# First layer: two output blocks as standard products and plain values; last layer: one line of linear-attention units with tied reads

## The chip, the cores and the metric

The kernel runs on one core of one Trainium2 chip. The metric is the device time of one execution in microseconds. It is given as the median of several runs; one further execution was taken with the hardware profiler, and the profile page and the trace describe that one.

## The reference

Two layers with the same shape work on 512 tokens of width 2048, all in float32. A layer normalises its rows, multiplies by one wide input matrix, and splits the result into a linear-attention group (4 heads, key width 128, value width 256, a forget gate), a chunked softmax-attention group (8 heads of 128, a relative bias) and a gate for each. The results are normalised for each head, gated, put side by side, multiplied by an output matrix, normalised, and added to the residual.

```
def hybrid_layer(x, w_in, w_out, ...):
    z = rmsnorm(x, g_pre) @ w_in
    gq, gk, gv, gg, ga, aq, ak, av, ag = split_columns(z)
    log_a = log_sigmoid(ga @ w_alpha + b_alpha) / 16
    o_gla = rmsnorm(gla_chunk_causal(gq, gk, gv, log_a), g_gla) * silu(gg)
    o_att = rmsnorm(chunk_band_attention(aq, ak, av, rel_bias), g_att) * silu(ag)
    return x + rmsnorm(concatenate([o_gla, o_att]) @ w_out, g_post)
```

The linear attention keeps a state for each head (128x256). For each chunk of 64 tokens the state is multiplied by a decay and the chunk's outer product of keys and values is added; the chunk's queries then read that new state.

## The kernel before

**Products.** Weights come as blocks of 512 columns: 14 input blocks and 4 output blocks in each layer. Each block is read in 8 chunks of 256 rows, as tiles of 128 x 1024 numbers. A float32 operand is split in a high part, rounded by ScalarE (L257), and a low part, the difference, made by VectorE (L263); a product is three matmuls: high by high, high by low, low by high. Two blocks together form a pair, which is multiplied by a Strassen-Winograd scheme (class `Pair`): seven products P1 to P7 in place of eight, each over 4 chunks. A product of one chunk is 12 matmuls of 128x512 (L523); the query and key pairs run feature-major, 24 of 128x256 (L508). The scheme needs sums of weight tiles (L246, L249, L269, on VectorE, in `Job.high` and `Job.low`) and sums S1 to S4 of the left operand. Those of the input side are made by `token_sums` and read back from memory as `sa`. A pair that is `early` runs P1 and P2 first and reads the lower weight tile again for P4; `second` pairs read their upper tile again for P5. A `seeded` pair copies finished partial results back to PSUM with ScalarE (L453, L547), so that TensorE goes on adding to them; one that isn't seeded combines them with VectorE.

`std_gemm` is the plain alternative: a block is multiplied chunk by chunk, with 6 matmuls for each chunk and each of the four token tiles, and each tile has its own PSUM bank. The last `lag` chunks are ordered tile by tile, so that the banks close one after another. No layer of the kernel before calls it: `PAIRED = (0, 1)` (L138) sends both layers to `paired_out` (L1577 on), which ends `layer`.

**Order of the work in a layer.** Three front pairs (gates and attention values), two query and key pairs with the attention heads beside them, the pair of linear-attention keys and queries, the value pair (`GV0, GV1`, P1 and P2 first), and then the output projection. In `paired_out` this is two pairs, W01 and W23: P1 and P2 of both, then the rest of W01, then the rest of W23. The sums of the output's left operand come from `paired_sums`: S1 and S3 stay in SBUF (`A["S1", c]`), S2 and S4 go through memory (`oS`). Some sums wait until the first output tile is evacuated (`"first"` in `issued`). The last output products are followed by the final rows (`finish_token`, L1557), which in the first layer are transposed (L731) to the next layer's operand by `prep_chunk`. `finish` starts when the low parts of named jobs are made.

**Side work.** Generators in `tasks` are advanced by `pump`, a number of steps after each product (`rate`); `delayed` holds steps to be taken some steps later; `beside(main, other, every)` advances `other` once in `every` steps of `main`. `ahead` loads the weight tiles up to five jobs ahead, fetches left sums up to four ahead, and makes the high and low parts three to four ahead. A scheduler orders the instructions of each engine from this order, and `issue_after(x)` makes an instruction follow `x` on its engine.

**Linear attention.** A `Unit` (L1274) is one head in one half of the tokens (p is 0 or 1). It takes the outer products (`outer`, L1294, four products tied by `issue_after`), the states (`states`, L1314 and L1316 on VectorE), the reads (`read`, L1330, four products, not tied), the norm, the gate (L1348) and the transposes (`turn`, L1358). The profile counts 8 instructions for the four outer products of a unit and 8 for its reads. The last state of a first half is kept in `ends` for the second half. As soon as one half of a value block is done, `gla_heads` takes that block's two heads through that half: four tasks of two units, one after the other, and each task overlaps its two units. The last task carries `paired_sums`.

**Queues.** SP issues the weights, the left operands, and in `load_parts` the sources of the sums; the POOL queue issues what is written to memory, the gain rows, and the residual rows.

Of the kernel before, what the change touches and what calls it, by code (L numbers as in the profile page):

```python
# [35 lines left out]
def hybrid_trunk(  # L36
# [13 lines left out]
    nc = tc.nc  # L50
# [20 lines left out]
    def slot(tag, shape, dtype=F32):  # L71
        return slots.tile([P] + shape, dtype, tag=tag, name=nm(tag))
# [19 lines left out]
    def aux():  # L92
        return ps_ax.tile([P, 512], F32, tag="ax", name=nm("ax"))
# [41 lines left out]
    W01 = (NB_IN, NB_IN + 1)  # L135
    W23 = (NB_IN + 2, NB_IN + 3)
    OUT = (W01[0], W23[0])
    PAIRED = (0, 1)  # L138
    C_IN, C_END = (0, 1, 2, 3), (2, 3, 0, 1)
    MIDDLE = (("P6", 0), ("P3", 0), ("P6", 1), ("P3", 1), ("P6", 2), ("P6", 3), ("P3", 2), ("P3", 3))  # L140

# [36 lines left out]
    class Job:  # L178
# [39 lines left out]
        def bring(self):  # L218
            k, c, p = self.kind, self.c, self.pair
            end = self.b0 in OUT  # L220
            name = LEFT.get(k)
            if self.a is not None:
                return
            src = (so_d if end else sa_d)[self.l].get((name, c))
            if end and name in ("S1", "S3"):
                return
            if src is None or p.get("direct") or p.get("second") and not end and (name, c) in RESIDENT:
                return
            until(lambda: (self.l, end, name, c) in made)
# [42 lines left out]
    for l in range(L):  # L272
        infos = [{"early": True, "direct": True}, {"early": True, "second": True}, {"early": True, "second": True}]
        infos_of.append(infos)
        for k, i in HEAD:
            stream += [Job(l, k, c, *FRONT[i], infos[i]) for c in C_IN]
        for (b0, b1), pr in zip(FRONT, infos):
            stream += [Job(l, k, c, b0, b1, pr) for k, c in early_rest(C_IN)]
        for b0, b1 in PAIRS:
            pr = {"early": b0 == GV0}  # L280
            order = early_head(C_IN) + early_rest(C_IN) if pr["early"] else PROD
            stream += [Job(l, k, c, b0, b1, pr) for k, c in order]
        if l in PAIRED:
# [36 lines left out]
    tasks = []  # L320
# [99 lines left out]
    class Pair:  # L420
# [60 lines left out]
        def operand(self, job, k, c):  # L481
            if job.a is not None:
                return job.a
            if self.end and k in ("P5", "P7"):
                until(lambda: (LEFT[k], c) in A)
                return A[LEFT[k], c]
            if k in ("P1", "P2", "P4") and (self.l, LEFT.get(k), c) not in S_on:
                key = {"P1": (0, 0, c), "P2": (1, 0, c), "P4": (1, 1, c)}[k]
                until(lambda: key in A)
                return A[key]  # L490
            until(lambda: (self.l, False, LEFT[k], c) in made)
            return S_on[self.l, LEFT[k], c]
# [292 lines left out]
    def make_sums(l, end, tags, parts, chunks=range(4), order=None):  # L785
# [4 lines left out]
        def add(name, c):  # L790
            a11, a12, a21, a22 = got[c]
            out, in0, in1, op = {
                "S1": (a22, a21, a22, ALU.subtract), "S3": (a21, a11, a21, ALU.subtract),
                "S2": (a22, a22, a11, ALU.subtract), "S4": (a12, a12, a22, ALU.add),
            }[name]
            with tc.issue_after(last_out[0] or last_state[0]) if end else nullcontext():
                nc.vector.tensor_tensor(out=out, in0=in0, in1=in1, op=op)

        def put(name, c):
# [89 lines left out]
    def layer(l):  # L889
# [379 lines left out]

        og, og_full, issued = {}, {}, {"outer": 0, "states": 0}  # L1270
        last_out[0] = None
        ends = slot("g1" if paired else "g3", [4, 256])

        class Unit:  # L1274
            def __init__(self, h, p, gv):
                self.h, self.p, self.gv, self.i = h, p, gv, issued["outer"]
                st = slot(f"g{9 + self.i % 2}", [4, 256])
                self.st = [st[:, q, :] for q in range(4)]
                if p == 0:
                    self.st[3] = ends[:, h, :]  # L1280
                self.prev = ends[:, h, :] if p else None

            def outer(self):
                h, p = self.h, self.p
# [38 lines left out]
            def read(self):  # L1323
                h, p = self.h, self.p
                self.ps_o = aux()
                for tt in range(2):
                    for cc in range(2):
                        q = 2 * tt + cc
                        n = 4 * p + q
                        nc.tensor.matmul(  # L1330
                            self.ps_o[cc * 64 : (cc + 1) * 64, tt * 256 : (tt + 1) * 256],
                            gqT[h // 2][:, h % 2, n * 64 : (n + 1) * 64], self.st[q],
                            start=True, stop=True,
                        )

            def norm(self):
                ss, self.r = sm(2), sm(2)
# [43 lines left out]
                if ("O", 0) in A:  # L1381
                    A[1, p, h] = op

        def gla_heads(specs):
            units = []

            def new(k):
                h, p = specs[k]
                units.append(Unit(h, p, [gv[h // 2, z] if (h // 2, z) in gv else None for z in range(2)]))
                units[-1].outer()  # L1390

            for _ in range(2 if paired else 4):
                yield
            new(0)
            yield
            units[0].states()
            yield
            for k in range(len(specs)):
                more = k < len(specs) - 1
                if more:  # L1400
# [5 lines left out]
                if more:  # L1406
# [7 lines left out]
                yield  # L1414

        def early_sums():
            while not {(p, h) for p in range(2) for h in (2, 3)} <= set(og):
                yield
            while not paired and issued["states"] < 8:
                yield  # L1420
            yield from output_sums(l, (2, 3))

# [44 lines left out]
                yield  # L1467

        gv = {}
        GV = {(0, 0): "g2", (1, 0): "g4", (1, 1): "g5", (0, 1): "g0"}  # L1470
        passed = set()
        op_att = {}

# [12 lines left out]

        def gv_consume(j, h, t, src, comb):
            if (j, h) not in gv:
                until(lambda: (4 if j or h else 0) in heads_done)
                gv[j, h] = slot(GV[j, h], [2, 512])  # L1490
            dst = gv[j, h][:, t, :]
            if comb is None:
                nc.scalar.activation(dst, src, AF.Copy, scale=inv_rms(l, 2 * h + t))
            else:
                comb(dst)
            if t:
                heads = gla_heads([(2 * j, h), (2 * j + 1, h)])
                if (j, h) == (0, 1):
                    heads = beside(heads, paired_sums(), 2) if paired else beside(heads, early_sums(), 3)
                tasks.append(heads)  # L1500

        values = Pair(l, PAIRS[3], gv_consume, early=True, seeded=True, x_bank=flip ^ 2)
        values.run(early_head(C_IN), rate=4, after=fetch_operands)
        values.open(flip ^ 2)
        values.run(early_rest(C_IN)[:-4], rate=4, after=fetch_operands)
        values.run(early_rest(C_IN)[-4:], rate=4, after=fetch_operands)
        A.clear()

        def operand_out(half, ch):
# [241 lines left out]
```

## Time and profile before

| what | us |
|---|---|
| median of 3 runs | 1634.35 (1633.36 to 1635.29) |
| the profiled execution's own time | 1636.54 |
| its span, first to last instruction | 1634.8 |
| TensorE busy | 1589.1 |
| VectorE busy | 1292.8 |
| ScalarE busy | 948.3 |
| POOL busy | 160.2 |

PE is TensorE's matmuls, PEld its weight loads, DVE is VectorE, ACT ScalarE, and SP the engine that only issues transfers. The profiled execution's own time has 1.7 us outside the span. A row of a view by windows gives the window (us from the start of the span), its length, the busy time and count of each engine, the granted share of TensorE's clock, the mean busy share of the DMA engines, and GB/s. A row of the timeline gives the start, the time taken, the engine, the source line, the operation and how many of them; in brackets is the idle time before it and what ended it. A row of the view of waits gives the total wait, how often, and the longest.

### The profile page before, as it was taken

The page shows a single profiled execution, that of the slowest core. Times are in us where ns is not written, and L with a number is a line of the kernel's source. Part 1 is how long each engine was busy: PE and PEld are TensorE (multiplying, and loading weights), DVE is VectorE, ACT ScalarE, POOL GpSimd, SP SyncE. Part 2 cuts the span into 40 slices and gives each one's busy share as a digit, 9 for nine tenths or more (in the row PEclk, how much of TensorE's full clock was granted, in tenths as well). Part 3 has the DMA queues.
Part 4 walks back from the last instruction along what each step waited for, and adds up shares of the span by engine and source line. Part 5 has one row for each costly group of instructions (what it writes and reads, how often), then busy time and mean ns, then how long its engine had stood idle before and what let it go on. Part 6 is the DMA issues. An engine that isn't in the chain of part 4 may idle for free.

```text
span 1634.8 us, 24266 instructions
## 1 busy us (share of the span) xinstructions
PE 1589.1 (97%) x8722; PEld 1340.2 (82%) x8722; DVE 1292.8 (79%) x1600; ACT 948.3 (58%) x1562; POOL 160.2 (10%) x282
## 2 busy tenths in 40 slices
PE   9999999999999999989899999999999999998896
PEld 6777889999988876767787888899999887766675
DVE  6878976877876787878878888868788767778788
ACT  8565544556676555645585555446657665466343
POOL 1131000000000001110122100000010010010101
PEclk9999999999999999999999999999999999999999
DMA  9999866858867587879769889768586756967795
GB/s 369 357 339 347 326 233 234 300 184 298 278 222 252 206 312 279 288 263 342 260 236 334 324 318 329 258 227 285 191 296 226 259 201 250 367 214 264 274 334 176
DMA packets 144890, 451.57 MB, mean 276 GB/s; under 512 B 15885, under 2 KB 35349, under 8 KB 144769
## 3 DMA queue, kind: packets, MB, share of 16 engines
q1 hardware_dynamic: 124640, 381.07, 66.3%
q0 software_dynamic: 19552, 67.99, 11.1%
q8 instruction: 69, 1.13, 0.3%
q10 hardware_dynamic: 576, 0.95, 0.2%
q14 instruction: 53, 0.43, 0.1%
HBM read 391.44 MB, written 57.43 MB: 275 GB/s over the span
## 4 chain that ended last, share of the span: by engine, by line
PE 78%; DMA 7%; issue 6%; DVE 6%; ACT 1%; POOL 1%; SPq 0%; POOLq 0%; DVEq 0%; ACTq 0%
PE mm L523 48%; PE mm L508 20%; DMA raw<-in_w_dram 3%; DVE wl L263 2%; PE ax L1124 2%; DMA H<-in_w_dram 2%; PE ax L1330 1%; DVE H L246 1%; PE ax L1107 1%; DMA sa<-oS 1%; PE ax L1294 1%; DMA sa<-A 1%; PE ax L1087 1%; PE ax L1086 1%; PE ax L1085 1%
## 5 line engine op out<-in xcount | busy, mean ns | idle before, releaser
L257 ACT CAST wh<-H 128x1024 fp32r<-128x1024 f32 x263 | 276.1, 1052 | 233.5 <-PE mm L523 96.3
L263 DVE TENSOR_TENSOR wl<-H,wh 128x1024 fp32r<-128x1024 f32 (+1 forms) x265 | 321.8, 1217 | 94.0 <-PE mm L523 40.6
L263 DVE TENSOR_TENSOR wl<-raw,wh 128x1024 fp32r<-128x1024 f32 x240 | 292.8, 1220 | 107.4 <-PE mm L523 45.9
L257 ACT CAST wh<-raw 128x1024 fp32r<-128x1024 f32 x240 | 252.5, 1053 | 199.2 <-PE mm L523 92.1
L523 PE MATMUL mm<-wh,sa 128*128 128x512 f32 x1088 | 350.5, 395 | 8.6 <-ACT mm L453 3.8
L523 PE MATMUL mm<-wh,a 128*128 128x512 f32 x1024 | 331.7, 396 | 2.7 <-ACT a L113 1.3
L523 PE MATMUL mm<-wh,g 128*128 128x512 f32 x1024 | 319.8, 391 | 0.2 <-ACT mm L547 0.2
L246 DVE TENSOR_TENSOR H<-H,raw 128x1024 f32<-128x1024 f32 x192 | 233.0, 1220 | 33.3 <-DMA raw<-in_w_dram 22.9
L523 PEld LDWEIGHTS mm<-wh,sa 128*128 128x128 f32 x1088 | 203.7, 189 | 58.4 <-ACT mm L453 5.3
L508 PE MATMUL mm<-sa,wh 128*128 128x256 f32 x1280 | 236.0, 285 | 0.0
L523 PEld LDWEIGHTS mm<-wh,a 128*128 128x128 f32 x1024 | 191.5, 188 | 52.9 <-issue 9.3
L523 PEld LDWEIGHTS mm<-wh,g 128*128 128x128 f32 x1024 | 193.0, 188 | 40.6 <-ACT mm L547 0.9
L523 PE MATMUL mm<-wl,sa 128*128 128x512 f32 x544 | 214.1, 394 | 3.2 <-DVE wl L263 3.2
L523 PE MATMUL mm<-wl,g 128*128 128x512 f32 x512 | 202.2, 395 | 9.9 <-DVE wl L263 9.7
L523 PE MATMUL mm<-wl,a 128*128 128x512 f32 x512 | 201.4, 394 | 1.8 <-DVE wl L263 1.8
L508 PEld LDWEIGHTS mm<-sa,wh 128*128 128x128 f32 x1280 | 199.5, 191 | 0.3
L508 PE MATMUL mm<-sa,wl 128*128 128x256 f32 x640 | 180.7, 283 | 0.0
L523 PEld LDWEIGHTS mm<-wl,g 128*128 128x128 f32 x512 | 96.5, 188 | 36.6 <-DVE wl L263 16.9
L523 PEld LDWEIGHTS mm<-wl,sa 128*128 128x128 f32 x544 | 102.5, 188 | 26.2 <-DVE wl L263 4.6
L508 PEld LDWEIGHTS mm<-sa,wl 128*128 128x128 f32 x640 | 122.3, 191 | 0.1
L523 PEld LDWEIGHTS mm<-wl,a 128*128 128x128 f32 x512 | 96.2, 188 | 24.4 <-DVE wl L263 4.0
L249 DVE TENSOR_TENSOR raw<-H,raw 128x1024 f32<-128x1024 f32 x72 | 87.8, 1219 | 11.1 <-DMA raw<-in_w_dram 10.9
(207 smaller groups left out, 1797.7 us busy)
## 6 DMA issues: line engine op xcount, KB each, us to landing
raw<-in_w_dram SPq DMA_DIRECT2D x360, 512.0 KB, 5.7
sa<-S SPq DMA_DIRECT2D x128, 512.0 KB, 4.6
H<-in_w_dram SPq DMA_DIRECT2D x71, 512.0 KB, 5.9
S<-g POOLq DMA_DIRECT2D x32, 512.0 KB, 5.8
g<-S SPq DMA_DIRECT2D x32, 512.0 KB, 5.2
sa<-A SPq DMA_DIRECT2D x32, 512.0 KB, 6.3
sa<-oS SPq DMA_DIRECT2D x32, 512.0 KB, 5.7
sg<-t POOLq DMA_DIRECT2D x32, 256.0 KB, 5.8
```

Source lines behind the costliest of these rows:

```text
L246: nc.vector.tensor_tensor(out=h, in0=h, in1=r, op=ALU.add)
L249: nc.vector.tensor_tensor(out=r, in0=h, in1=r, op=ALU.subtract)
L257: last_cast[0] = nc.scalar.copy(self.wh, src).ins
L263: last_low[0] = nc.vector.tensor_tensor(out=self.wl[:, kk, :], in0=self.src[:, kk, :], in1=self.wh[:, kk, :].bitcast(F32), op=ALU.subtract ...
L508: nc.tensor.matmul(dst, lhs[:, kk, f], a[:, part, tok], start=(fresh and kk == 0 and m == 0 and ft % 2 == 0), stop=(c == self.last and kk ...
L523: mm = nc.tensor.matmul(out_ps[t], a[:, part, tok], rhs[:, kk, :], start=(fresh and kk == 0 and m == 0), stop=(c == self.last and kk == 1 ...
L1085: nc.tensor.matmul(ps[:, :n], self.qh[:, t], self.kh[:, :n], start=True, stop=False)
L1086: nc.tensor.matmul(ps[:, :n], self.qh[:, t], self.kl[:, :n], start=False, stop=False)
L1087: nc.tensor.matmul(ps[:, :n], self.ql[:, t], self.kh[:, :n], start=False, stop=True)
L1107: nc.tensor.transpose(ps[:, j * P : (j + 1) * P], self.prob[i][:, j * P : (j + 1) * P], ident)
L1124: nc.tensor.matmul(o, self.pt[i][:, j * P : (j + 1) * P], av[hd // 4, j // 2][:, j % 2, (hd % 4) * P : (hd % 4 + 1) * P], start=(j == 0), ...
L1294: mm = nc.tensor.matmul(self.ps_u[cc][:, tt * 256 : (tt + 1) * 256], kd[p][r, tt, hk], self.gv[p][r, tt, hv], start=True, stop=True,).ins
```

## The change

In the first layer:
- `PAIRED` is now `(1,)`, so the output projection goes through the second half of `layer`: block 0 by `std_gemm` over four token tiles, block 1 by `std_gemm` over the first two, then the pair W23 (early, not seeded), then block 1 again over the last two tiles. Block 1's weights are read twice. In the order of the work this puts the second half of block 1 after the pair.
- The left sums are made by `output_sums`: all four go through memory, and their sources are read on SP. The attention operand of the second token half comes through memory, and is read twice.
- The value pair is plain: P1, P5, P6 and P3, P7, P2, P4, with the partial results combined on VectorE.
- `gla_heads` takes one block's two heads through both halves: four units in one chain, heads 2 and 3 after P7, heads 0 and 1 after P4. Heads 0 and 1 thus run beside block 0.

In the last layer:
- One generator, `gla_line`, takes all eight units in the order in which their values come. In each turn it issues a new unit's outer products and then the older unit's reads; `paired_sums` runs beside it from the start.
- The four reads of a unit are tied by `issue_after`, as the outer products already are.

```diff
-    PAIRED = (0, 1)
+    PAIRED = (1,)
...
-            if end and name in ("S1", "S3"):
+            if end and self.l in PAIRED and name in ("S1", "S3"):
...
-            pr = {"early": b0 == GV0}
+            pr = {"early": b0 == GV0 and l in PAIRED}
...
-            with tc.issue_after(last_out[0] or last_state[0]) if end else nullcontext():
+            with tc.issue_after(last_state[0]) if end else nullcontext():
...
                 self.ps_o = aux()
+                mm = None
                 for tt in range(2):
                     for cc in range(2):
...
-                        nc.tensor.matmul(
+                        with tc.issue_after(mm) if paired and mm else nullcontext():
+                            mm = nc.tensor.matmul(
...
-        def gla_heads(specs):
+        def gla_heads(j, gv):
             units = []
             def new(k):
-                h, p = specs[k]
+                h, p = 2 * j + k // 2, k % 2
...
+        def gla_line():
+            n, older = 0, None
+            while n < 8 or older is not None:
+                newer = None
+                if units_due:
+                    h, p = units_due.pop(0)
+                    newer = Unit(h, p, [gv.get((h // 2, z)) for z in range(2)])
+                    newer.outer()
+                    n += 1
+                elif older is None:
+                    yield
+                    continue
+                yield
+                if older is not None:
+                    older.read()
+                yield
+                if newer is not None:
+                    newer.states()
+                yield
+                if older is not None:
+                    older.norm()
+                yield
+                yield
+                if older is not None:
+                    older.gate()
+                    delayed.append([4, older.turn])
+                yield
+                yield
+                older = newer
...
         def early_sums():
             while not {(p, h) for p in range(2) for h in (2, 3)} <= set(og):
                 yield
-            while not paired and issued["states"] < 8:
-                yield
...
-            if t:
-                heads = gla_heads([(2 * j, h), (2 * j + 1, h)])
-                if (j, h) == (0, 1):
-                    heads = beside(heads, paired_sums(), 2) if paired else beside(heads, early_sums(), 3)
-                tasks.append(heads)
+            if t and paired:
+                if (j, h) == (0, 0):
+                    tasks.append(beside(gla_line(), paired_sums(), 2))
+                delayed.append([2, lambda: units_due.extend([(2 * j, h), (2 * j + 1, h)])])
+            elif h and t:
+                heads = gla_heads(j, [gv[j, p] for p in range(2)])
+                tasks.append(heads if j else beside(heads, early_sums(), 3))
...
+        if paired:
+            values = Pair(l, PAIRS[3], gv_consume, early=True, seeded=True, x_bank=flip ^ 2)
...
+        else:
+            fast_gemm(l, PAIRS[3], gv_consume, rate=4, after=fetch_operands, x_bank=flip ^ 2)
```

More of the change, by code (lines that the diff above doesn't have):

```diff
@@ L483, in operand @@
                 return job.a
-            if self.end and k in ("P5", "P7"):
+            if self.end and self.l in PAIRED and k in ("P5", "P7"):
                 until(lambda: (LEFT[k], c) in A)
@@ L1271, in layer, with __init__ @@
         last_out[0] = None
-        ends = slot("g1" if paired else "g3", [4, 256])
+        ends = slot("g1", [4, 256]) if paired else None
         class Unit:
-            def __init__(self, h, p, gv):
+            def __init__(self, h, p, gv, prev=None):
                 self.h, self.p, self.gv, self.i = h, p, gv, issued["outer"]
@@ L1278, in __init__ @@
                 self.st = [st[:, q, :] for q in range(4)]
-                if p == 0:
+                self.prev = prev.st[3] if prev else None
+                if paired and p == 0:
                     self.st[3] = ends[:, h, :]
-                self.prev = ends[:, h, :] if p else None
+                elif paired:
+                    self.prev = ends[:, h, :]
             def outer(self):
@@ L1329, in read @@
                         n = 4 * p + q
[L1330 to L1334, printed above, removed]
+                        with tc.issue_after(mm) if paired and mm else nullcontext():
+                            mm = nc.tensor.matmul(
+                                self.ps_o[cc * 64 : (cc + 1) * 64, tt * 256 : (tt + 1) * 256],
+                                gqT[h // 2][:, h % 2, n * 64 : (n + 1) * 64], self.st[q],
+                                start=True, stop=True,
+                            ).ins
             def norm(self):
@@ L1382, in turn @@
                     A[1, p, h] = op
-        def gla_heads(specs):
+        def gla_heads(j, gv):
             units = []
             def new(k):
-                h, p = specs[k]
-                units.append(Unit(h, p, [gv[h // 2, z] if (h // 2, z) in gv else None for z in range(2)]))
+                h, p = 2 * j + k // 2, k % 2
+                units.append(Unit(h, p, gv, units[-1] if p else None))
                 units[-1].outer()
-            for _ in range(2 if paired else 4):
+            for _ in range(4):
                 yield
@@ L1397, in gla_heads @@
             yield
-            for k in range(len(specs)):
-                more = k < len(specs) - 1
-                if more:
+            for k in range(4):
+                if k < 3:
                     new(k + 1)
@@ L1405, in gla_heads @@
                 yield
-                if more:
+                if k < 3:
                     units[k + 1].states()
@@ L1414, in gla_heads @@
                 yield
+        units_due = []
+        def gla_line():
[27 more added lines that the diff above has]
+                older = newer
         def early_sums():
             while not {(p, h) for p in range(2) for h in (2, 3)} <= set(og):
-                yield
-            while not paired and issued["states"] < 8:
                 yield
@@ L1469, in layer @@
         gv = {}
-        GV = {(0, 0): "g2", (1, 0): "g4", (1, 1): "g5", (0, 1): "g0"}
+        GV = {(0, 0): "g2" if paired else "g0", (1, 0): "g4", (1, 1): "g5", (0, 1): "g0" if paired else "g1"}
         passed = set()
@@ L1488, in gv_consume @@
             if (j, h) not in gv:
-                until(lambda: (4 if j or h else 0) in heads_done)
+                until(lambda: (4 if j or h or not paired else 0) in heads_done)
                 gv[j, h] = slot(GV[j, h], [2, 512])
@@ L1495, in gv_consume @@
                 comb(dst)
-            if t:
-                heads = gla_heads([(2 * j, h), (2 * j + 1, h)])
-                if (j, h) == (0, 1):
-                    heads = beside(heads, paired_sums(), 2) if paired else beside(heads, early_sums(), 3)
-                tasks.append(heads)
[L1502 to L1506, printed above, removed]
+            if t and paired:
[7 more added lines that the diff above has]
+            values = Pair(l, PAIRS[3], gv_consume, early=True, seeded=True, x_bank=flip ^ 2)
+            values.run(early_head(C_IN), rate=4, after=fetch_operands)
+            values.open(flip ^ 2)
+            values.run(early_rest(C_IN), rate=4, after=fetch_operands)
+        else:
+            fast_gemm(l, PAIRS[3], gv_consume, rate=4, after=fetch_operands, x_bank=flip ^ 2)
         A.clear()
```

## The prediction

> **What bounds the kernel now.** I read the page's busy times first, then the chain of waits, then the stretches of single weight products, and then the waits inside the stretches that were too long.
>
> ```profile
> span 1634.8 us, 24266 instructions
> PE 1589.1 (97%) x8722; PEld 1340.2 (82%) x8722; DVE 1292.8 (79%) x1600; ACT 948.3 (58%) x1562; POOL 160.2 (10%) x282
> ```
>
> TensorE is busy 97% of the span. What one product matmul costs is read from the chain where nothing else interferes:
>
> ```profile
> 882.19 81.91 PE mm L523 x360
> 964.55 92.48 PE mm L523 x408
> ```
>
> 92.48 / 408 = 0.2267 us for each 128x512 matmul. A product of one chunk is 12 of them (2.72 us), one product over its four chunks 48 (10.9 us). With this ruler each stretch of the first layer's output projection can be compared with its work. The next rows count the line 523 matmuls alone; the columns are the window, its length, PE busy (count), weight loads (count), granted clock, DMA share and GB/s. The first five are the first layer, the last three the same places in the last layer.
>
> ```profile
> 686.80:702.00 15.20, 11.86 (x49) 8.81 (x48) 1.00 0.61 225
> 702.00:729.50 27.50, 23.73 (x98) 17.74 (x97) 1.00 0.89 326
> 751.20:764.80 13.60, 11.62 (x50) 8.80 (x49) 1.00 1.02 411
> 764.80:797.40 32.60, 32.60 (x145) 27.01 (x144) 1.00 0.83 271
> 797.40:818.80 21.40, 11.41 (x50) 8.80 (x48) 0.92 0.68 255
> 1493.70:1510.40 16.70, 12.25 (x50) 8.79 (x49) 1.00 0.64 237
> 1510.40:1538.80 28.40, 24.45 (x97) 18.83 (x96) 0.94 0.86 318
> 1562.80:1578.10 15.30, 12.79 (x50) 10.11 (x49) 0.89 0.90 356
> ```
>
> (A count one or two over 48, 96 or 144 is a neighbour's matmul at the edge.) The window 764.80:797.40 has no loss: 144 x 0.2267 = 32.6. The first has P5 of pair W01, 48 matmuls in 15.2 us instead of 10.9: 4.3 lost. P6 and P3 of W01 lose 27.5 - 21.8 = 5.7. P5 of W23 loses 13.6 - 10.9 = 2.7. Together 12.7 us. The last layer loses 5.8 + 6.6 + 4.4 in the same three places, so the cause is in the way a paired projection works. Who is waited for in the first layer between 686 and 765, and how busy VectorE is there (PE, PEld, DVE, ACT, POOL):
>
> ```profile
> PE mm L523 <- DVE wl L263: 5.7, 5, 1.5
> PE mm L523 <- ACT mm L453: 1.9, 1, 1.9
> PE mm L523 <- DMA sa<-oS: 1.3, 1, 1.3
> 686.80:729.50 42.70, 35.58 (x146) 26.55 (x145) 34.97 (x39) 20.08 (x28) 5.37 (x10) 1.00 0.79 290
> 729.50:764.80 35.30, 33.32 (x146) 26.78 (x145) 33.39 (x35) 19.52 (x30) 2.67 (x5) 1.00 0.91 327
> ```
>
> VectorE is busy 68.4 of 78 us: it makes the low parts and the weight sums, and the sums of the left operand, all at once. TensorE waits for it, for the scalar copies that seed the banks (L453), and for operands from memory. The stretch 797.40:818.80 is the way into the second layer:
>
> ```profile
> 808.80 1.47 PE L731 MATMUL ax<-cst,g 128*128 128x128 f32 x12
> 815.60 3.39 PE L731 MATMUL ax<-cst,g 128*128 128x128 f32 x16 [5.33 <-DVE g L741]
> ```
>
> Here TensorE has no products left and waits 5.33 us for the normalised rows; then 16 transposes take 3.39 us, 0.21 each, where the 12 before took 0.12 each. That is the lower clock (0.92 mean in this window): another 1.7 us. So 7.0 us go at the border of the layers.
>
> **The change, part by part.**
>
> *Two blocks standard in layer 0.* A pair is 7 products x 4 chunks x 12 = 336 matmuls for two blocks; standard, a block is 8 chunks x 4 token tiles x 6 = 192, two are 384. So 48 matmuls are added: 48 x 0.2267 = +10.9 us. Nothing can hide them, since TensorE is the queue they stand in. The Trainium skill (Perfetto Trace Analysis, Identifying the Most-Contended Engine) says that matmul busy time is a poor measure of headroom and that weight-load busy share is a better one. By that rule the 82% would leave 18% of the span, and the sum would lose its +10.9 term. The trace does not bear that out here: in the full window 764.80:797.40 the loads are 27.0 of 32.6 us (83%), and the pitch stays at 0.2267, so this way gets no chance of its own.
>
> *What that takes away.* The W01 pair's weight sums (P5, P6, P7 and P4, four chunks each) and four low parts go:
>
> ```profile
> L246 DVE TENSOR_TENSOR H<-H,raw 128x1024 f32<-128x1024 f32 x192 | 233.0, 1220 | 33.3 <-DMA raw<-in_w_dram 22.9
> ```
>
> 20 x 1.22 = 24.4 us less on VectorE, and no seeds in this projection. The left sums S1 to S4 spread over block 0 and the first half of block 1 instead of 80 us of pairs. I take the 10.0 us of W01's stalls as gone, and the 2.7 of W23's P5 too (its weight loads double no more: the pair is no longer the "second" one): -12.7. It would stay at 0 if the same wait returned at the new pair; that is a rival.
>
> *The border.* The last step is now the second half of block 1, 96 matmuls = 21.8 us after the new pair's P4, and the first two token rows are finished and transposed during it. Before, only P7's tail and P4 stood over that work. The wait of 5.33 us and the half clock after it have more than twice the cover, so -7.0. If the cover failed, 7.0 would come back whole.
>
> *What memory must carry.* This is the term with no row of its own, since standard blocks don't run in the kernel before. The sizes and latencies:
>
> ```profile
> raw<-in_w_dram SPq DMA_DIRECT2D x360, 512.0 KB, 5.7
> sa<-oS SPq DMA_DIRECT2D x32, 512.0 KB, 5.7
> oS<-g POOLq DMA_DIRECT2D x16, 512.0 KB, 5.0
> a<-fa SPq DMA_DIRECT2D x8, 256.0 KB, 4.3
> t<-in_g_post_dram POOLq DMA_DIRECT2D x12, 256.0 KB, 6.3
> fg<-t POOLq DMA_DIRECT2D x8, 256.0 KB, 6.0
> ```
>
> From block 1's first half to its second, TensorE has 96 + 336 + 96 matmuls, 119.7 us, and some 3.4 us of transposes: 123 us. In them fall 40 weight tiles (21.0 MB), 16 left sums read (8.4), 8 written (4.2), the sources of the last 8 (8 x 256 KB, 2.1), the attention operand fetched a second time (2.1), the residual rows (4.2), four gain rows (1.0) and half of x_mid (2.1): 45.1 MB, less about 2 MB of residual rows that start in block 0. That is 43 / 123 = 350 GB/s of demand. The nearest row is the first layer's front, where weights, columns and sums move together; below it a stretch with less traffic:
>
> ```profile
> 83.70:175.10 91.40, 89.83 (x386) 71.25 (x385) 1.00 0.92 334
> 893.20:1056.90 163.70, 163.70 (x724) 135.54 (x723) 140.02 (x133) 91.85 (x112) 14.67 (x27) 1.00 0.86 305
> ```
>
> In the first, 384 matmuls are 87.0 us of work in 91.4, and 30.5 MB over 87.0 us is a demand of 351 GB/s: 4.4 us lost. In the second, 720 matmuls are 163.2 of 163.7: nothing lost at 305. Scaled, 4.4 / 87.0 x 123 = +6.2 us of new stalls. The bounds: nothing, if the 411 GB/s of 751.20:764.80 were available throughout (45.1 MB in 110 us); 15 us, if all of it went at the 326 GB/s of 702.00:729.50 (138 us). The Trainium skill (DMA: Bandwidth & Descriptors, Where 436 GB/s comes from) has the memory side bind at about 358 GB/s for a core. By that the term would be 45.1 / 0.358 - 123 = +3; the 411 row is above that limit, so the trace doesn't confirm it as a ceiling.
>
> *Queues.* Layer 0's sources are now read on SP, whose next entries are weights. A source waits for the linear attention's write (fg, 6.0 us). In block 0 a weight tile lasts 24 x 0.2267 = 5.4 us and four are buffered, so this costs nothing there; in block 1 (2.7 us a tile, 10.9 buffered) at most a couple of us, inside the bounds above. S1 and S3 go through memory as S2 and S4 do now. The final units of heads 0 and 1 now run in block 0, whose last two chunks need them: 33 us after its start, plus the units' own matmuls. Their pipeline of 34 to 39 steps at 1.7 steps per 1.36 us is done about then, each unit a chunk ahead of its use: nothing, and a few us if the last unit is late.
>
> *Values plain in layer 0.* Same 336 matmuls, four weight loads less, no seeds. The key and query pair already runs in this order. Nothing, either way under 1 us.
>
> *Last layer.* The reads (L1330) of a unit are now tied in order, as the outer products (L1294) already are. Rows of both:
>
> ```profile
> 567.46 2.00 PE L1294 MATMUL ax<-g,g 64*128 64x256 f32 x16
> 575.32 1.94 PE L1330 MATMUL ax<-g,g 128*64 128x256 f32 x14
> 1442.98 0.49 PE L523 MATMUL mm<-wh,a 128*128 128x512 f32 x1
> 1443.41 0.65 PE L1330 MATMUL ax<-g,g 128*64 128x256 f32 x2
> 1443.99 0.49 PE L523 MATMUL mm<-wl,a 128*128 128x512 f32 x1
> ```
>
> In a burst a read takes 0.12 us (575.32 row: 13 steps from first to last start in 1.56). Split in twos, 1442.98 to 1443.99 holds one product and two reads, 0.47 of work in 1.01 us: a break costs about 0.5. In the last layer two units are split in four and two are split once, 3 + 3 + 1 + 1 = 8 breaks too many: 8 x 0.44 = -3.5 us, taking a little under the row. One line of eight units takes 7 steps a unit where two overlapping units took 16 steps; the last unit comes about 7 steps, 1.75 chunks or 5 us, later. The sums of chunks 0 and 1 wait anyway for the first output tile, 12 chunks into the projection, so I cost that at nothing; if sums are pushed into the busy stretch 1493.70:1538.80, up to +3. Bounds -4 to +3.
>
> **Sum**, against the profiled execution's own 1636.54 us: +10.9 - 12.7 - 7.0 + 6.2 - 3.5 = -6.1, so 1630.4. The median of the runs is 2.2 us under the profiled one, so 1628 us, 0.4% faster. About 0.2% (3.3 us) is what can be told from no change here.
>
> **The rivals.** (1) *Memory becomes the bound of layer 0's last three steps.* For it: the demand of 350 is over every long stretch of the trace, and writes and 256 KB pieces are mixed in. Against: 411 GB/s for 13.6 us. If 315 GB/s is what it gets (between the 305 and 326 rows), 45.1 MB take 143 us, the term is 20 instead of 6.2, and the sum is +7.7: 1642. It turns the result to slower than before once the term passes 12.3, so below 333 GB/s. (2) *The stalls only move.* The new pair still makes sums, low parts and evacuations together, with its partial results now combined by VectorE rather than seeded; the front of the last layer shows such pairs running without loss, W23's P5 shows one that doesn't. If half of the 12.7 stays, the sum is +0.3 and the time 1634.6. (3) *The line doesn't do what it says:* ties order the reads but products still come between, and the later last unit costs 3 us. Then -3.5 becomes +3, the sum +0.4, and the time 1635. The unbroken outer products, tied the same way, speak against it.
>
> **How the numbers follow.** Forecast (faster by over 3.3 us) 0.50; rivals 2 and 3, and half measures between, 0.20 within 3.3 us; rival 1 and what of block 0's late units may add to it 0.30. Low end: no new stall and -4 in the last layer, 10.9 - 12.7 - 7.0 - 4 = -12.8: 1621.5. High end: rival 1, 1642.
>
> **What would show it.** Right: two stretches of standard products in layer 0, 192 and 96 matmuls at 0.2267, then the pair, then 96 more; no wait of over 1 us for L263 in them; no 5 us wait before L731 and no clock drop there; L1330 in eights in the last layer; from the first layer's values to the second layer's first product about 2.6 us less than before (10.9 - 12.7 - 7.0 + 6.2). Wrong: long waits of line 257, 246 or the standard matmuls for weights or oS, with a DMA share over 0.9 at 315 GB/s or less; the last layer's losses of 5.8, 6.6 and 4.4 us grown.

## The result and the profile after

The new kernel takes 1620.28 us (median of 4 runs, 1620.19 to 1621.84), against 1634.82 for the kernel before in the same comparison: ratio 0.9911, 95% interval 0.9894 to 0.9928, or 14.5 us less. The forecast was faster, 1628, with a low end of 1621.5: the direction is right, and the time is 1.2 us under the low end of the range. The profiled execution's own time is 1620.26. The head of its page, and the shares of its chain of waits (the second fence has the kernel before's):

```profile
span 1618.5 us, 24386 instructions
PE 1585.6 (98%) x8770; PEld 1347.6 (83%) x8770; DVE 1275.7 (79%) x1590; ACT 934.7 (58%) x1548; POOL 174.2 (11%) x292
PE 88%; issue 4%; DMA 4%; DVE 2%; ACT 1%; POOL 0%; SPq 0%; POOLq 0%; DVEq 0%; ACTq 0%
```

```profile
PE 78%; DMA 7%; issue 6%; DVE 6%; ACT 1%; POOL 1%; SPq 0%; POOLq 0%; DVEq 0%; ACTq 0%
```

There are 48 matmuls more, and TensorE's share of the chain has gone from 78% to 88%: what went is waiting. Where it went, from the timelines of TensorE in the two profiles:

| stretch | before, us | after, us | difference |
|---|---|---|---|
| start to the first layer's value pair | 535.9 | 534.5 | -1.4 |
| value pair to the second layer's first product | 282.9 | 269.9 | -13.0 |
| from there to the last layer's value pair | 522.7 | 523.1 | +0.4 |
| from there to the end of the span | 293.3 | 291.0 | -2.3 |

The first and third rows hold work that is unchanged. Over all the profiles shown here they run from 534.0 to 537.6 and from 522.3 to 525.6, so a difference of 2 or 3 us in these rows means nothing. The second row is steadier: it is 269.9 in all six profiles that have this first layer unaltered. The 13.0 us are the first layer's change. The view by windows of the new kernel, in the first layer: block 0 with the units of heads 0 and 1, the first half of block 1, the pair from P5 to P4, and everything from block 1's first half to the next layer (PE, PEld, DVE, ACT, POOL, clock, DMA share, GB/s):

```profile
625.00:681.10 56.10, 56.10 (x281) 42.61 (x280) 36.43 (x63) 27.98 (x63) 17.86 (x29) 1.00 0.81 285
681.10:702.90 21.80, 21.80 (x98) 18.03 (x97) 16.78 (x20) 11.48 (x15) 2.25 (x5) 1.00 1.04 398
724.70:779.10 54.40, 54.40 (x242) 45.06 (x241) 49.11 (x51) 29.06 (x39) 8.90 (x6) 1.00 0.93 345
681.10:804.40 123.30, 123.30 (x561) 102.42 (x561) 104.26 (x118) 73.26 (x108) 17.28 (x25) 1.00 0.91 344
```

TensorE is never idle in them. In the second and third rows 96 matmuls in 21.8 us and 240 in 54.4 are 0.227 us each. VectorE is still 90% busy in the pair (49.1 of 54.4), but nothing waits for it. At the border the same two groups of transposes as before now stand like this in TensorE's timeline:

```profile
784.10 1.47 PE L731 MATMUL ax<-cst,g 128*128 128x128 f32 x12
790.42 1.91 PE L731 MATMUL ax<-cst,g 128*128 128x128 f32 x16
```

There is no idle time before the 16, and they take 0.12 us each instead of 0.21, so the lower clock is gone too.

The last layer has a new wait, just before P5 of pair W01. The view of waits, the line 523 matmuls by windows (P2, P5, P6 and P3 of W01; P5 of W23), POOL's timeline, and VectorE's:

```profile
PE mm L523 <- DVE g L1573: 4.1, 1, 4.1
```

```profile
1464.50:1480.20 15.70, 11.48 (x50) 8.80 (x48) 1.00 0.92 321
1480.20:1494.10 13.90, 13.12 (x48) 10.13 (x49) 0.88 0.30 115
1494.10:1525.30 31.20, 23.98 (x97) 18.89 (x97) 0.89 0.78 287
1547.30:1561.90 14.60, 11.81 (x50) 8.80 (x49) 1.00 1.02 402
```

```profile
1461.20 0.71 POOL L582 TENSOR_TENSOR sm<-sm,cst 128x2 f32<-128x2 f32 x1 [2.48 <-ACT sm L586]
1462.06 1.13 POOL L1560 DMA_DIRECT2D t<-in_g_post_dram  x2
```

```profile
1479.35 1.28 DVE L1573 TENSOR_TENSOR g<-mm,t 128x512 f32<-128x512 f32 x2
```

P2 loses 4.8 us. P5 adds into the banks that hold W23's first output tile. That tile is complete at 1464.5, but VectorE multiplies it by its gain row, and so empties the banks, only at 1479.35. The gain row was asked for at 1462.06, on POOL's queue right behind the last unit's norm (L582), and such a row lands about 5.8 us later. So the row is there by about 1468; for the other 11 us VectorE has other work in front of the evacuation, weight sums and low parts above all.

### The profile page after: what moved, and what is told of

The parts are those of the page before. It is cut to its first block, busy times and chain, and to the rows that moved or that the text cites. A ratio compares the mean times of both kernels' runs of the same rounds, so it can differ in the third digit from the quotient of the medians.

```text
span 1618.5 us, 24386 instructions
## 1 busy us (share of the span) xinstructions
PE 1585.6 (98%) x8770; PEld 1347.6 (83%) x8770; DVE 1275.7 (79%) x1590; ACT 934.7 (58%) x1548; POOL 174.2 (11%) x292
## 4 chain that ended last, share of the span: by engine, by line
PE 88%; issue 4%; DMA 4%; DVE 2%; ACT 1%; POOL 0%; SPq 0%; POOLq 0%; DVEq 0%; ACTq 0%
PE mm L523 52%; PE mm L508 20%; PE mm L394 5%; PE ax L1124 2%; DMA raw<-in_w_dram 2%; DMA H<-in_w_dram 1%; DVE wl L263 1%; PE ax L1296 1%; PE ax L1107 1%; PE ax L1334 1%; PE ax L523 1%; PE ax L717 1%; PE ax L1087 1%; PE ax L1086 1%; PE ax L1085 1%
## 5 line engine op out<-in xcount | busy, mean ns | idle before, releaser
L263 DVE TENSOR_TENSOR wl<-H,wh 128x1024 fp32r<-128x1024 f32 (+1 forms) x253 | 307.8, 1219 | 93.2 <-PE mm L523 38.6
L523 PE MATMUL mm<-wh,g 128*128 128x512 f32 x928 | 289.2, 391 | 4.1 <-DVE g L1573 4.1
L523 PE MATMUL mm<-wh,a 128*128 128x512 f32 x864 | 279.3, 396 | 3.0 <-ACT a L113 1.1
L246 DVE TENSOR_TENSOR H<-H,raw 128x1024 f32<-128x1024 f32 x176 | 213.8, 1222 | 27.4 <-DMA raw<-in_w_dram 18.9
L523 PEld LDWEIGHTS mm<-wh,g 128*128 128x128 f32 x928 | 175.0, 189 | 40.7 <-issue 4.5
L523 PEld LDWEIGHTS mm<-wh,a 128*128 128x128 f32 x864 | 161.5, 188 | 42.8 <-issue 4.3
L523 PE MATMUL mm<-wl,g 128*128 128x512 f32 x464 | 182.1, 393 | 4.2 <-DVE wl L263 4.2
L523 PE MATMUL mm<-wl,a 128*128 128x512 f32 x432 | 169.6, 394 | 1.2 <-DVE wl L263 1.2
L523 PEld LDWEIGHTS mm<-wl,a 128*128 128x128 f32 x432 | 81.2, 188 | 19.9 <-DVE wl L263 3.3
L508 PE MATMUL mm<-a,wh 128*128 128x256 f32 x512 | 94.5, 285 | 0.0
```

The costliest lines, as they stand in the source:

```text
L246: nc.vector.tensor_tensor(out=h, in0=h, in1=r, op=ALU.add)
L263: last_low[0] = nc.vector.tensor_tensor(out=self.wl[:, kk, :], in0=self.src[:, kk, :], in1=self.wh[:, kk, :].bitcast(F32), op=ALU.subtract ...
L508: nc.tensor.matmul(dst, lhs[:, kk, f], a[:, part, tok], start=(fresh and kk == 0 and m == 0 and ft % 2 == 0), stop=(c == self.last and kk ...
L523: mm = nc.tensor.matmul(out_ps[t], a[:, part, tok], rhs[:, kk, :], start=(fresh and kk == 0 and m == 0), stop=(c == self.last and kk == 1 ...
```

## The experiments

**The first layer alone** (`first_only`). The last layer gets back the four tasks of two units, with the reads not tied:

```diff
-                if (j, h) == (0, 0):
-                    tasks.append(beside(gla_line(), paired_sums(), 2))
-                delayed.append([2, lambda: units_due.extend([(2 * j, h), (2 * j + 1, h)])])
+                heads = gla_pairs([(2 * j, h), (2 * j + 1, h)])
+                tasks.append(beside(heads, paired_sums(), 2) if (j, h) == (0, 1) else heads)
...
-                        with tc.issue_after(mm) if paired and mm else nullcontext():
+                        with tc.issue_after(mm) if False else nullcontext():
```

> The first layer changed as in the new kernel, the last layer as before: its value halves start pairs of units, reads not tied. Theory: the first layer alone brings nearly all, 13.0 us between its value pair and the next layer's first product (10.9 more work, 12.8 less waiting in the projection, 6.9 less at the border, 4.4 less for the linear-attention units, and no new wait for memory), so 1621 to 1622 us, ratio 0.992. Rival: the first layer brings only the 2.6 us that the prediction gave it and the last layer the rest, so about 1632 us, ratio 0.998.

Measured: 1617.67 us, ratio 0.9906 (0.9889 to 0.9922). The first layer's change alone brings all of the gain.

**The last layer alone** (`last_only`). The kernel before, with `gla_line` and the ties in the last layer.

```diff
+            if t and last:
+                if (j, h) == (0, 0):
+                    tasks.append(beside(gla_line(), paired_sums(), 2))
+                delayed.append([2, lambda: units_due.extend([(2 * j, h), (2 * j + 1, h)])])
...
```

> The first layer as before (both output pairs paired, values early), the last layer with the one line of units and tied reads. Theory: 1.5 to 2.5 us faster, about 1632.5 us, ratio 0.9985: some 4 us less for the units and a new wait of 4 to 5 us before P5 of pair W01, partly given back after it. Rival: the last layer brought what the first did not, 10 us or more, about 1623 us.

Measured: 1633.64 us, ratio 1.0011 (0.9998 to 1.0024). It isn't faster, so the theory's small gain fell with the rival. In its profile the units cost the last layer less, and P2 of W01 loses 3.7 us, where the kernel before lost 0.2.

**Ties without the line** (`first_ties`). As the first kernel, but with `if paired and mm` left in.

> The first layer changed, the last layer with the old pairs of units but tied reads: the line is left out. Theory: the reads come in eights, which saves the breaks, 3 to 4 us, and since the last unit is not later the wait before P5 of pair W01 is not there: 1617 to 1619 us, 2 to 3 us under the kernel with the line. Rival: the line and not the ties is what saves the breaks: 1621.5 us, as with the first layer alone.

Measured: 1615.65 us, ratio 0.9897 (0.9880 to 0.9914). But this is no second kernel. It builds to the same program as the one without ties, so the 2.0 us between the two are what two samples of one program differ by. The last layer's reads, still tied, in TensorE's timeline:

```profile
1426.97 0.65 PE L1334 MATMUL ax<-g,g 128*64 128x256 f32 x2
1427.97 0.65 PE L1334 MATMUL ax<-g,g 128*64 128x256 f32 x2
1428.97 0.65 PE L1334 MATMUL ax<-g,g 128*64 128x256 f32 x2
1429.97 0.65 PE L1334 MATMUL ax<-g,g 128*64 128x256 f32 x2
```

They come in twos, as before: a tie sets an order, which the reads had anyway, and lets products in between. The new kernel with its ties taken out also comes to the same program. So the ties do nothing. In the first layer, with no ties at all, the reads of the new kernel come in eights. There the chain of four units issues them at another time; that this is the reason is argued, not shown:

```profile
607.18 1.14 PE L1296 MATMUL ax<-g,g 64*128 64x256 f32 x8
608.24 1.08 PE L1334 MATMUL ax<-g,g 128*64 128x256 f32 x8
615.60 1.14 PE L1296 MATMUL ax<-g,g 64*128 64x256 f32 x8
616.66 1.08 PE L1334 MATMUL ax<-g,g 128*64 128x256 f32 x8
```

**Standard blocks with the old values and units** (`first_early`). The kernel before, with `PAIRED = (1,)` and only what that needs:

```diff
-            if end and name in ("S1", "S3"):
+            if end and self.l in PAIRED and name in ("S1", "S3"):
...
-            if self.end and k in ("P5", "P7"):
+            if self.end and self.l in PAIRED and k in ("P5", "P7"):
...
```

> The kernel before with only the two output blocks of the first layer made standard: its values stay early and seeded, its units stay in four tasks of two. The last layer is as before. Theory: the blocks bring 10.9 - 12.8 - 6.9 = -8.8 us, and the 4.4 us of cheaper units come from the chain of four units with the plain values, so they are missing: 1626 us, ratio 0.9945. Rival: the units are cheaper because half of them now run beside a standard block, whatever the order of the values: 1621 to 1622 us, ratio 0.992.

Measured: 1621.80 us, ratio 0.9932 (0.9912 to 0.9953). From the value pair to the second layer its profile has 273.7 us: 9.2 less than before, 3.8 more than the new kernel. The blocks bring 9 us, and plain values with chains of four, which weren't tried apart, bring the other 4, as the theory said. The intervals of this ratio and of `first_only`'s overlap, so the split rests on the profiles.

**The border** (`unsplit`). Block 1 of the first layer runs once, over all four token tiles, before the pair, and the first rows are finished from P7 on:

```diff
-        std_gemm(l, NB_IN + 1, (0, 1), OO, operand_out, out_evac(1), rate=0.6, lag=2)
+        std_gemm(l, NB_IN + 1, range(NT), OO, operand_out, out_evac(1), rate=0.6, lag=1)
...
-        std_gemm(l, NB_IN + 1, (2, 3), OO, operand_out, last_evac, ...)
...
```

> The new kernel, but in the first layer block 1 is multiplied once over all four token tiles, before the pair, so the pair is the last step; the first rows are finished from P7 on, as in the kernel before. Theory: the standard products behind the pair are what covers the border. Without them the wait before the transposes and the lower clock come back, 5 to 7 us: 1625 to 1627 us. Rival: the border is short because the pair no longer runs with the sums beside it; then the time stays at 1620 us or falls a little, since 8 weight tiles and 4 operand tiles less are read.

Measured: 1626.59 us, ratio 0.9936 (0.9912 to 0.9960), about 4 us over the new kernel's ratio, with intervals that overlap. The time lies in the theory's range, but the mechanism doesn't hold: in the profile the way from the value pair to the second layer is 271.5 us, only 1.6 longer than in the new kernel. The window of P4, now the last step, and the 16 transposes:

```profile
791.70:807.30 15.60, 15.02 (x81) 12.24 (x80) 15.60 (x20) 9.42 (x17) 5.57 (x5) 1.00 0.96 352
```

```profile
805.02 1.91 PE L730 MATMUL ax<-cst,g 128*128 128x128 f32 x16
```

TensorE is busy 15.0 of 15.6 us. There is no 5 us wait and no lower clock, though nothing but the pair covers the border. The window is 15.6 us where the kernel before took 21.4. So most of the border's 7 us doesn't come from the 96 matmuls that were put there.

**The border's other cause** (`before_gains`). The kernel before, with one gain row of each pair, in both layers, asked for earlier:

```diff
-                    elif (k, c) == ("P4", C_END[0]):
+                    elif (k, c) == ("P7", C_END[0]):
                         gains[n] = load_gain(n, nc.gpsimd)
```

> The kernel before with one thing moved: in both layers' paired projections the gain row that each pair's P4 needs is asked for 4 products earlier, after P7's first chunk instead of P4's. Theory: at the border TensorE waits 5.33 us because VectorE stands at a gain row that was asked for at 807.06 and is used at 813.12; with the row there, the transposes follow at once, the lower clock does not come, and 5 to 7 us go at the border: 1627 to 1630 us. Rival: the border is long because nothing but P4 covers the last rows; then the wait only changes its name and the time stays within 2 us.

Measured: 1627.82 us, ratio 0.9963 (0.9949 to 0.9977): 6 us faster than the kernel before, with one request moved in each of four pairs. Its transposes at the border:

```profile
800.60 1.47 PE L731 MATMUL ax<-cst,g 128*128 128x128 f32 x12
806.95 1.03 PE L731 MATMUL ax<-cst,g 128*128 128x128 f32 x8
808.75 1.03 PE L731 MATMUL ax<-cst,g 128*128 128x128 f32 x8
```

The idle time is gone, and from P4 to the second product of the next layer the loss is 6.4 us instead of 13.2; in the new kernel it is 6.3. What held the border was the gain row: VectorE stood at it for 1.9 us, and the evacuation that the transposes needed was queued behind. The standard form asks for those rows on SP, before the pair. That this is what makes the border short in the new kernel and in `unsplit` is the likely reading; no run delays the request there. The result bears on the whole change. From the value pair to the second layer this profile has 273.3 us, as short as the 273.7 of `first_early`: in this stretch the paired blocks with their gain rows in time do as well as the standard ones, without 48 more products. The whole time isn't as good (ratio 0.9963 against 0.9932, intervals that overlap a little), and no run joins the moved request to the other parts of the change.

**More traffic** (`mem2`). Each of the 8 left sums of chunks 0 and 1 in the first layer is written twice more, to memory that nothing reads:

```diff
...
+            if end and l == 0 and c in (0, 1):
+                for _ in range(2):
+                    nc.gpsimd.dma_start(spare_d.pop(), flat(op))
```

> The new kernel with two more writes, to scratch memory that nothing reads, of each of the 8 left sums of chunks 0 and 1 in the first layer: 16 more transfers of 512 KB, 8.4 MB, between block 0 and the last standard step. Theory: memory still had room; the stretch carried 42.4 MB in 123.3 us (344 GB/s) without a wait, and its first 21.8 us ran at 398 GB/s; 50.8 MB need 123 us at 412 GB/s, so a loss of 0 to 5 us. Rival: the limit is near 350 GB/s and the new kernel stands at it; then 8.4 MB cost 24 us, 1644 us.

Measured: 1638.37 us, ratio 1.0014 (1.0002 to 1.0027), 17 us over the new kernel's ratio. Both expectations missed. The windows from block 1's first half on, and the whole stretch:

```profile
682.90:704.60 21.70, 21.70 (x97) 18.00 (x96) 16.71 (x20) 11.53 (x15) 5.29 (x10) 1.00 1.04 405
704.60:729.60 25.00, 21.97 (x97) 17.84 (x96) 15.04 (x18) 11.85 (x20) 6.41 (x13) 0.99 1.03 416
729.60:747.20 17.60, 14.66 (x48) 10.61 (x49) 12.88 (x12) 5.14 (x5) 1.07 (x2) 0.83 1.03 418
682.90:819.80 136.90, 129.10 (x561) 103.31 (x560) 105.06 (x118) 72.91 (x108) 20.32 (x40) 0.98 0.95 369
```

For 64 us memory moves 405 to 418 GB/s at a share of 1.03 to 1.04, and TensorE starts to wait 22 us in. The stretch is 13.6 us longer (136.9 to 123.3). So the ceiling is above 400, not near 350, and the new kernel runs its 123 us at 344 under it. Its first half of block 1 ran at 398 and a share of 1.04 without any wait of TensorE, so even a full memory need not cost time at once. The 13.6 us need not be the price of 8.4 MB alone. ScalarE waits 4.7 us, before it makes a sum, for one of the added writes, which points at a buffer that the write still reads; and TensorE's longest wait here, of 3.0 us, is for ScalarE:

```profile
ACT g L114 <- DMA spare<-g: 4.7, 1, 4.7
PE mm L524 <- ACT wh L258: 3.0, 1, 3.0
```

The two costs were not tried apart. The Trainium skill (Perfetto Trace Analysis, Roofline) gives about 435 GB/s as the ceiling of a single core's 16 DMA engines, with 358 as the share when two cores read. The trace fits the first, since the one core here moved 418.

**The last layer's gain rows** (`gains_first`).

```diff
+                    if (n, k, c) == (0, "P1", C_END[0]):
+                        gains[2], gains[0] = load_gain(2, nc.gpsimd), load_gain(0, nc.gpsimd)
                     if (n, k, c) == (0, "P1", C_END[3]):
-                        gains[2], gains[0] = load_gain(2, nc.gpsimd), load_gain(0, nc.gpsimd)
```

> The new kernel with the first two gain rows of the last layer's projection asked for at the first product of pair W01 instead of its fourth. Theory: the wait of 4.5 us before P5 of pair W01 is for the bank that the pair W23's first output tile holds; that tile is evacuated 15 us late because its gain row was asked for behind the last unit's norm on the POOL queue. With the row there in time the wait goes, and the time falls by 2 to 5 us, to 1615 to 1618 us. Rival: VectorE's own queue holds the evacuation back, whatever the row; then nothing changes, 1620 us.

Measured: 1618.04 us, ratio 0.9884 (0.9867 to 0.9901), 4.4 us under the new kernel's ratio; the two intervals overlap a little, but this one lies clear of the second measurement of the new kernel below (0.9907 to 0.9938). P2, and then P6 and P3 of W01, and the wait in the latter:

```profile
1465.40:1476.80 11.40, 11.32 (x50) 8.97 (x49) 1.00 0.82 276
1492.30:1527.20 34.90, 25.52 (x97) 20.18 (x96) 0.83 0.70 258
```

```profile
PE mm L523 <- DMA sa<-oS: 9.4, 1, 9.4
```

The wait before P5 is gone (11.4 us for 48 matmuls, 0.5 lost), as the theory said. Part of it comes back as a wait for a sum that goes through memory. Here too asking for the gain row earlier removes the wait, though the row was not what VectorE stood at: with the earlier request VectorE takes the evacuation at 1471.87, ahead of weight work that it did first in the new kernel. The second wait was not followed further.

**The line against the tasks, again** (`new_again`, `first_again`; no edit).

> The new kernel once more, beside the next one on the same chip, to set the last layer's line apart. Theory: the line saves some 4 us of breaks in the last layer and gives them back in the later wait before P5 of pair W01, so this and the kernel with the first layer changed alone lie within 3 us of each other. Rival: the line costs or brings more than 3 us.

> The first layer changed alone, once more. Theory: within 3 us of the new kernel, 1616 to 1620 us. Rival: more than 3 us away from it.

Measured on one chip: 1621.68 us, ratio 0.9923 (0.9907 to 0.9938), with the line; 1616.18 us, ratio 0.9894 (0.9875 to 0.9914), without. That is 4.7 us apart, outside the theory's 3 us, but the intervals overlap, and the first two measurements of these kernels (0.9911 and 0.9906) were 0.8 us apart by the ratios. The profiles tell more. Without the line, P2, P5, P6 and P3 of W01 and P5 of W23 stand like this, and the gain rows are asked for earlier:

```profile
1466.00:1476.80 10.80, 10.80 (x49) 8.97 (x48) 1.00 0.73 237
1476.80:1494.20 17.40, 13.47 (x50) 9.86 (x50) 0.90 0.61 230
1494.20:1520.30 26.10, 23.22 (x98) 17.81 (x97) 1.00 0.88 335
1542.00:1556.30 14.30, 11.84 (x50) 8.82 (x49) 1.00 1.02 403
```

```profile
1458.96 1.17 POOL L1590 DMA_DIRECT2D t<-in_g_post_dram  x2 [0.35 <-DMA raw<-in_w_dram]
```

P2 loses nothing, with the rows asked for 7.0 us before W23's P2 ends, where the line had 2.4. From the last value pair to the end, the three profiles without the line (`first_only`, `first_ties`, `first_again`, one program) have 286.5, 286.6 and 286.6 us; with it, 291.0 and 293.0. The line's value pair with its units is cheaper by some 3 us, and the waits behind it cost 7 to 9 more. So the line costs 4 to 6 us there.

**Both layers in the new form** (`both_std`).

```diff
-    PAIRED = (1,)
+    PAIRED = ()
```

> The last layer takes the first layer's new form too: two output blocks standard, plain values, units in chains of four. Theory: the last layer's paired projection still loses 22.6 us in waits, which the standard form does not have; it costs 10.9 us of products, and the end of the kernel keeps its tail: 1607 to 1613 us, 8 to 12 us under the new kernel. Rival: the last layer has no next layer to cover, and with no paired sums its tail after the last products grows: no gain, 1620 us or more.

Measured: 1605.24 us, ratio 0.9802 (0.9784 to 0.9821): 30 us under the kernel before and 18 under the new one by the ratios, more than the theory gave it. This beats both kernels. From the last value pair to the end it takes 274.9 us, against 286.5 in `first_only`. The head of its page, and the last layer: values and block 0, then the first half of block 1 with the pair, and the last half:

```profile
span 1603.0 us, 24514 instructions
```

```profile
1418.50:1474.70 56.20, 56.20 (x282) 42.63 (x281) 36.50 (x63) 27.84 (x63) 17.86 (x29) 1.00 0.80 285
1474.70:1572.60 97.90, 97.90 (x433) 81.11 (x432) 83.04 (x89) 51.95 (x70) 13.13 (x12) 1.00 0.94 350
1572.60:1594.50 21.90, 21.90 (x97) 17.84 (x95) 14.37 (x16) 7.21 (x11) 1.63 (x3) 1.00 0.46 161
```

TensorE is busy without a gap to its last product, and the end behind it is 8.5 us.

## Why the prediction was right and wrong, step by step

- *Two blocks standard, +10.9 us.* Right. The 384 matmuls run at 0.2267 us, and none was hidden.
- *W01's stalls and W23's P5, -12.7 us.* Right. No product of the first layer's projection waits, and block 0 needed no margin for the late units. With the border this gives -8.8 for the blocks; `first_early` has -9.2. Against the paired form with its gain rows in time (`before_gains`) the trade is about even: there the same places lose 11.2 us.
- *The border, -7.0 us.* The size is right (10.5 us over the products in P4's stretch before, 3.6 after, all transposes). The reason is wrong, so the size is luck: the prediction had "more than twice the cover". `unsplit` has no such cover and no such wait, and `before_gains` removes the wait in the kernel before by asking for one row earlier. The row was in the wait list (VectorE waits 1.9 us for `t<-in_g_post_dram`), and the prediction stopped one step short of it, at the transposes' wait for VectorE. It also didn't ask where the standard form requests it.
- *What memory must carry, +6.2 us.* This is the step that failed first. The demand was right: 350 GB/s worked out, 344 measured. The price was wrong: it measured 0. The prediction scaled "4.4 us lost" at 334 GB/s in the first layer's front, as if that were a rate limit. Cut into pieces of 10 us, that row doesn't bear it out: its fullest piece (133 to 143, 413 GB/s, share 1.03) loses nothing, while the piece before it (302 GB/s, share 0.83) loses 0.6 us of TensorE's time. With the same code the new kernel's profile loses 2.3 us there. TensorE's waits in the row are for VectorE's low parts and a scalar copy; VectorE in turn waits for weight tiles at times, so why the row loses time stays open. `mem2` shows what memory can carry: 405 to 418 GB/s, as in the row 751.20:764.80 that the prediction held to be the far bound.
- *The units in the first layer.* Costed at nothing, measured -4.4 us. This is the second step that failed, and the one that puts the time under the range: the low end already had no stall for memory. Beyond the matmuls of the value pair and the projection, 31.2 us of TensorE went on attention and units before and 26.8 after, for the same instructions. The prediction had priced a break at 0.5 us and then applied it to the last layer alone. Counted the same way, the first layer has 18 interruptions by outer products and reads before, 22.6 us in all, and 12 after, 18.2 us; that is the whole difference.
- *Last layer, -3.5 us.* Wrong, for both reasons given. The ties change nothing (rival 3 had this right). What does bring the last units' reads into eights is the line, and it saves some 3 us there. But the last unit's delay, "costed at nothing" because the sums wait anyway, isn't free: the gain rows are queued behind that unit's norm on POOL. The step didn't ask what stands behind a moved instruction on its queue. The line as a whole measured about +2 (`last_only`) to +6.

In sum: -6.1 forecast in the prediction's terms; with 0 for memory and -4.4 for the units it is -16.7, and with the last layer as this pair of profiles has it (-2.3 for -3.5), -15.5, near the 16.3 between the spans, of which 1.4 lie in the front. That the low end is only 1.2 us off is luck in part: its -4 for the last layer rests on ties that do nothing.

What stays open: in the three profiles with the first layer changed and without the line, the last layer's output products lose about 15.3 us, where the same order lost 20 in the kernel before and 18 in `before_gains`. The last layer's accumulators lie in the other pair of banks there. But they do in `first_early` too, which lost 17, so the banks alone don't explain it.

## What to carry to other kernels

More arithmetic in a plain order can beat a fast scheme that doesn't keep its engine fed: with both layers standard, 21.8 us of added products are part of the fastest kernel here. But the trade has to be set against the fast scheme with its waits mended. In the first layer 10.9 us of products took away 20 us of waiting, and 7 of the 20 hung on a request that could have been moved instead. Before a wait is put down to missing cover, follow it to its last releaser: two of the long waits here, 5.3 and 4.1 us, went when a 256 KB row was asked for earlier, and moving such requests was worth 6 us. A rate read where an engine waits is no limit by itself: cut the stretch, and see whether the time is lost where memory is fullest.

## What the runs showed of the hardware

What an interruption of TensorE's stream of 128x512 products costs depends on how the small products of the linear attention come. Two reads between products add 0.67 to 0.77 us for 0.24 us of work at the 0.12 us of a long burst; eight in a row add 1.11 us for 0.96 (timelines of the kernel before and the new kernel). So the same eight reads cost 2.9 to 3.0 us in four twos and 1.1 in one eight. One core moved 405 to 418 GB/s for 64 us between memory and SBUF, with writes among the reads (`mem2`). And one program measured on the same chip in the same comparison gave 1617.67 and 1615.65 us, which is as large as some of the effects here.
